# One-hot rows of the expert gates in four wide VectorE instructions, and six PSUM banks for the first expert product

## The chip, the cores and the metric

The kernel runs on one core of a Trainium2 chip. A core has a matrix engine (TensorE; PE in the rows, its weight loads PEld), three engines for elementwise work (VectorE or DVE, ScalarE or ACT, GpSimd or POOL) and a queue that issues DMAs (SyncE or SP). Each engine works through its own instructions strictly in order, and semaphores make one engine wait for another. Matmuls write to PSUM, which the kernel uses as eight banks of 128 x 512 float32. The metric is device time of the whole program in microseconds (us); lower is better.

## What is computed

The program is four layers one after another on 256 tokens of width 1024: a retention layer, a gated spatial layer, an attention layer and a delta-rule layer. The first two are each followed by a feed-forward layer with 16384 small experts, and the change lies in that feed-forward layer, which therefore runs twice. Cut to what matters:

```python
def peer_ffn(h, w_query, sub_keys, expert_u, expert_v):
    q = (ht @ w_query).reshape(T, 8, 2, 128)
    scores = einsum('thpd,hpkd->thpk', q, sub_keys)         # 128 keys per half
    s_top, i_top = top_k(scores, 16)
    cand = s_top[:, :, 0, :, None] + s_top[:, :, 1, None, :]
    best, pos = top_k(cand, 16)                             # 16 of 256 pairs per head
    expert_idx = i_top_0[a] * 128 + i_top_1[b]              # first index, second index
    gates = softmax(best)
    a = gelu(einsum('tkd,td->tk', expert_u[expert_idx], x)) * gates
    return einsum('tk,tkd->td', a, expert_v[expert_idx])
```

## The kernel before, in words

The kernel doesn't gather experts. It computes the product of the tokens with all 16384 rows of `expert_u` (the first expert product), multiplies by a gate matrix that is zero where an expert was not chosen, and multiplies by all of `expert_v` (the second). In `peer`, the first product is a loop over 128 blocks `i` of 128 experts. A block's weights are two **pieces** of four 128 x 128 tiles each. A piece arrives by DMA as float32 in `stage` (two buffers of four pieces each), is rounded by ScalarE to `whi` (line 143, "the cast"), and the remainder `wlo` is formed by VectorE, or by GpSimd for a part of the pieces (line 145). TensorE then makes three products per tile: `whi` with the tokens' high part, `whi` with their low part, `wlo` with their high part (lines 402 to 404). So a piece is 12 matmuls of 256 columns and a block is 24. A `stage` buffer is free for the next DMA when the last remainder of its four pieces is done. Eight pieces of `whi` and `wlo` can be held while the choice of experts runs, four afterwards (`closing.close()` gives back the extra buffers). GpSimd makes every second remainder up to there, then every fourth.

A block's sum lies in a PSUM bank, `acc`. ScalarE takes it out with a gelu to `gs` (line 1023), and every second block `gs` is spilled to DRAM. Before the change, `self.bank()` turns over two banks, `b0` and `b1`, so that the first matmul of a block needs the gelu of the block two before it. ScalarE's order for one block is: cast, cast, gelu, with the casts belonging to later blocks.

Beside the first product runs `choose`, a generator that is called for a little work after every block (`self.step`). It finds the top 16 of the scores and of the pairs, expands positions to indices with long bf16 operations of 2048 elements per partition (lines 931 to 940, "the expansion", once for each half of the tokens), and then builds the gate matrix four tokens at a time: 64 **groups** per layer, about six of them in every seven blocks. For a token, the gate matrix is a product of two one-hot matrices over its 128 choices: rows of the first index, and rows of the second index times the gate, the gate split in two float16 parts. In the kernel before that takes three VectorE instructions of 128 elements per token (lines 965 and 967), 12 per group, then eight matmuls of 128 columns (line 970) into a long-lived bank, and one ScalarE instruction that takes the bank out (line 972). `oh` has two buffers, so the first one-hot instruction of a group waits for the matmuls of the group two before. After the loop, the second product takes banks `b2` to `b5` for its sums.

The order on each engine is static: a scheduler lays the instructions down when the program is built, and may move a remainder in between one-hot instructions.

Of the kernel before, what the change touches and what calls it, by code (L numbers as in the profile page):

```python
# [14 lines left out]
HF = mybir.dt.float16  # L15
# [3 lines left out]
ALU = mybir.AluOpType  # L19
# [4 lines left out]
P = 128  # L24
D = 1024
KC = D // P
T = 256
# [25 lines left out]
NK = 128  # L53
# [268 lines left out]
class Kernel:  # L322
# [538 lines left out]
    def choose(self, scores, big, work, chosen, closing):  # L861

        nc = self.nc
        s16 = big.tile([P, 2, 16, TOPK], F32, tag="s16", name="s16")
        ix = big.tile([P, 2, 16, TOPK], U32, tag="ix", name="ix")
        i12 = chosen.tile([P, 2, T], HF, tag="i12", name="i12")
        gp = chosen.tile([P, 2, T], HF, tag="gp", name="gp")
# [9 lines left out]

        line = chosen.tile([P, NK], HF, tag="line", name="line")
        self.tc.keep_in_program_order(nc.vector.tensor_copy(line, self.const("iota")))
        for m in range(16):  # L880
            while m not in scores:
                yield -1
            for t in range(2):
                scratch = work.tile([P, P], F32, tag="scr", name="scr")
                self.top16(s16[:, t, m], ix[:, t, m], scores[m][:, t * P:(t + 1) * P], scratch)
                yield 1000
        ixb = big.tile([P, 2, 2, TOPK, PEER_H], BF, tag="ixb", name="ixb")
        nc.vector.tensor_copy(ixb, ix.rearrange("p t (h u) a -> p t u a h", u=2))
        iota = big.tile([P, TOPK, P], BF, tag="iota16", name="iota16")
# [3 lines left out]
        for t in range(2):  # L893
# [34 lines left out]
            for u in range(2):  # L928
# [4 lines left out]
                    op=ALU.is_equal)  # L933
                yield 1200
                nc.vector.tensor_tensor(eq, eq, ixb[:, t, u, :, None].to_broadcast([P, TOPK, TOPK, PEER_H]),
                                        op=ALU.mult)
# [22 lines left out]
        for t4 in range(T // 4):  # L959
            ts = slice(4 * t4, 4 * t4 + 4)  # L960
            acc = self.long_bank()
            oh = chosen.tile([P, 4, 3, NK], HF, tag="oh", name="oh", bufs=2)
            for u in range(4):
                t = slice(4 * t4 + u, 4 * t4 + u + 1)
                nc.vector.tensor_scalar(oh[:, u, 0], line, i12[:, 0, t], None, op0=ALU.is_equal)  # L965
                for w in range(2):
                    nc.vector.tensor_scalar(oh[:, u, 1 + w], line, i12[:, 1, t], gp[:, w, t], op0=ALU.is_equal,  # L967
                                            op1=ALU.mult)
                for w in range(2):
                    nc.tensor.matmul(acc[:, u * P:(u + 1) * P], oh[:, u, 0], oh[:, u, 1 + w], start=w == 0,  # L970
                                     stop=w == 1, skip_group_check=True)
            nc.scalar.activation(gates[:, :, ts], acc.rearrange("p (t i) -> p i t", t=4), AF.Copy,
                                 scale=1.0 / GATE_SCALE)
            yield 1400

    def peer(self, layer, later=()):
        nc = self.nc
        with ExitStack() as ctx:
            io = self.pool("peerio", bufs=2, ctx=ctx)
            chosen = self.pool("peersel", ctx=ctx)  # L980
# [27 lines left out]
            w = self.stream(f"peer_query{layer}", KC * 16)  # L1008
# [4 lines left out]
            self.rate = US  # L1013

            w = Weights(self, self.ins[f"peer_u{layer}"], NK * KC)
            for i in range(NK):
                acc = self.bank()[:, :T]
                for k in range(KC):
                    self.mm3(acc, w.tile(i * KC + k), (self.hi[:, k, :T], self.lo[:, k, :T]), k == 0, k == KC - 1)
                self.tick()  # L1020
                if i % 2 == 0:
                    gs = io.tile([P, 2 * T], F32, tag="gs", name="gs").rearrange("p (a b) -> p a b", a=2)
                nc.scalar.activation(gs[:, i % 2], acc, AF.Gelu_apprx_tanh)  # L1023
                if i % 2:
                    nc.scalar.dma_start(spill[i // 2], gs)
                self.step(self.rate)
# [4 lines left out]
            w = Weights(self, self.ins[f"peer_v{layer}"], NK * KC)  # L1031
# [4 lines left out]
            ts = slice(META, L) if layer else slice(0, T)  # L1036
# [6 lines left out]
            for i in range(NK):  # L1043
                if i % 2 == 0:

                    a = (io if i else chosen).tile([P, 2 * T], F32, tag="gs" if i else "oh", name="gs", bufs=2)
                    a = a.rearrange("p (a b) -> p a b", a=2)
# [679 lines left out]
```

## Time and profile before

| | |
|---|---|
| time, median of 3 runs | 3218.7 us (3213.13 to 3223.79) |
| the profiled execution | 3223.57 us, of which the span 3221.8 us |
| TensorE matmul busy | 3081.6 us, 96% of the span, granted clock 0.975 on average |
| VectorE busy | 2410.0 us, 75% |
| ScalarE busy | 1774.3 us, 55% |
| GpSimd busy | 526.2 us, 16% |
| first product, layer 0: first and last gelu start | 328.1 and 750.2 us |
| first product, layer 1 | 1439.4 and 1860.6 us |
| one-hot instructions, layer 0: first and last start | 427.0 and 725.2 us (line 965) |
| one-hot instructions, layer 1 | 1538.4 and 1835.7 us (line 965) |

Busy time of TensorE is modelled up to each matmul's end, and neighbouring matmuls overlap. Whether TensorE went at full pace is therefore better seen from the number of matmuls that a stretch holds than from its busy time. [...] VectorE's average over the span says little, since the stages differ: in the slices of the span that hold the one-hot instructions it is busy nine tenths or more.

### The profile page before, as it was taken

Reading aid. Unit: us, or ns where it says so; the run is one execution under the profiler, and the core shown is the slowest. Engines: PE = TensorE matmul, PEld = TensorE weight load, DVE = VectorE, ACT = ScalarE, POOL = GpSimd, SP = SyncE. Lnnn points to the kernel's source line nnn. Section 1 sums busy time; section 2 is a strip of 40 time slices with the busy share of each in tenths; the row PEclk is TensorE's granted clock in tenths of the full one; section 3 lists DMA queues with packets and bytes.
Section 4 is the critical chain, followed back from the end, with each engine's and each line's share of the span. In section 5 each row is a group of like instructions: output and inputs, shape, how many; then the busy total and the mean of one; then the engine's idle time right before and its main releaser. Section 6 shows DMA issues by size and latency. Waiting matters only on the chain. (4 is left out here: it accounts for less than half of the span.)

```text
span 3221.8 us, 63744 instructions
## 1 busy us (share of the span) xinstructions
PE 3081.6 (96%) x24317; PEld 2932.2 (91%) x24317; DVE 2410.0 (75%) x5694; ACT 1774.3 (55%) x3495; POOL 526.2 (16%) x476
## 2 busy tenths in 40 slices
PE   6999999999999999999999999999999998999998
PEld 5899999999999978999999999999677998898898
DVE  7777979996777687678899877666556965744783
ACT  4566555555555455555555555556456656824763
POOL 1213431110000003234321200000001001133101
PEclk8999999999999999999999999999899999989999
DMA  6655555558777765455555576665323543310453
GB/s 256 243 189 180 198 196 193 187 182 283 260 260 266 269 229 210 157 179 211 188 193 186 203 277 232 234 231 182 110 76 106 197 171 134 118 40 28 145 191 110
DMA packets 119779, 604.14 MB, mean 188 GB/s; under 512 B 14136, under 2 KB 15336, under 8 KB 61488
## 3 DMA queue, kind: packets, MB, share of 16 engines
q1 hardware_dynamic: 98496, 556.84, 48.8%
q10 hardware_dynamic: 19008, 35.72, 3.0%
q0 software_dynamic: 1968, 7.51, 0.7%
q8 instruction: 190, 3.11, 0.4%
q14 instruction: 117, 0.96, 0.1%
HBM read 565.38 MB, written 34.64 MB: 186 GB/s over the span
## 5 line engine op out<-in xcount | busy, mean ns | idle before, releaser
L402 PE MATMUL bank<-hi,whi 128*128 128x256 f32 (+1 forms) x5968 | 1725.4, 289 | 42.0 <-ACT gs L1023 17.5
L404 PE MATMUL bank<-hi,wlo 128*128 128x256 f32 (+1 forms) x5968 | 1707.5, 286 | 32.5 <-DVE wlo L145 30.2
L403 PE MATMUL bank<-lo,whi 128*128 128x256 f32 (+1 forms) x5968 | 1699.3, 285 | 1.2 <-DVE lo L379 1.2
L143 ACT CAST whi<-stage 128x512 fp32r<-128x512 f32 x1780 | 1077.0, 620 | 1051.7 <-PE bank L403 740.5
L145 DVE TENSOR_TENSOR wlo<-stage,whi 128x512 fp32r<-128x512 f32 x1566 | 1084.6, 707 | 468.0 <-ACT whi L143 452.1
L402 PEld LDWEIGHTS bank<-hi,whi 128*128 128x128 f32 x5968 | 1140.5, 191 | 62.1 <-ACT gs L1023 19.0
L404 PEld LDWEIGHTS bank<-hi,wlo 128*128 128x128 f32 x5968 | 1138.0, 191 | 52.2 <-DVE wlo L145 48.8
L403 PEld LDWEIGHTS bank<-lo,whi 128*128 128x128 f32 x5968 | 1139.0, 191 | 4.9 <-DVE lo L379 2.2
L145 POOL TENSOR_TENSOR wlo<-stage,whi 128x512 fp32r<-128x512 f32 x214 | 306.3, 1433 | 725.0 <-ACT whi L143 717.7
L967 DVE TENSOR_SCALAR oh<-line,i,gp 128x128 f16<-128x128 f16 x1024 | 337.5, 372 | 0.0
L403 PE MATMUL bank<-zl,whi 128*128 128x272 f32 (+1 forms) x736 | 211.3, 287 | 1.0 <-DVE zl L379 1.0
L402 PE MATMUL bank<-zh,whi 128*128 128x272 f32 (+1 forms) x736 | 211.7, 288 | 0.0
L404 PE MATMUL bank<-zh,wlo 128*128 128x272 f32 (+1 forms) x736 | 211.2, 287 | 0.0
L965 DVE TENSOR_SCALAR oh<-line,i 128x128 f16<-128x128 f16 x512 | 150.8, 295 | 0.0
L185 POOL TENSOR_TENSOR sqa<-sqa,sq 128x272 f32<-128x272 f32 (+1 forms) x36 | 30.0, 834 | 692.3 <-ACT sq L183 692.3
L403 PEld LDWEIGHTS bank<-zl,whi 128*128 128x128 f32 x736 | 140.2, 190 | 1.8 <-DVE zl L379 1.4
L402 PEld LDWEIGHTS bank<-zh,whi 128*128 128x128 f32 x736 | 140.1, 190 | 0.7 <-issue 0.4
L404 PEld LDWEIGHTS bank<-zh,wlo 128*128 128x128 f32 x736 | 139.8, 190 | 0.2 <-issue 0.2
L1049 DVE TENSOR_TENSOR gs<-gs,gates 128x512 f32<-128x512 f32 x128 | 88.1, 688 | 55.8 <-DMA gs<-spill 55.5
L1023 ACT ACTIVATE gs<-bank 128x256 f32<-128x256 f32 x256 | 96.8, 378 | 8.0 <-PE bank L404 7.9
L379 DVE TENSOR_TENSOR lo<-gs,hi 128x512 fp32r<-128x512 f32 x126 | 86.4, 686 | 0.4
L378 ACT CAST hi<-gs 128x512 fp32r<-128x512 f32 x126 | 77.9, 618 | 15.1 <-DVE gs L1049 15.0
(432 smaller groups left out, 3114.8 us busy)
## 6 DMA issues: line engine op xcount, KB each, us to landing
stage<-in_peer_u SPq DMA_DIRECT2D x128, 1024.0 KB, 4.8
stage<-in_peer_v SPq DMA_DIRECT2D x128, 1024.0 KB, 5.0
adaw<-in_ada_w SPq DMA_DIRECT2D x96, 512.0 KB, 4.9
stage<-in_ffn_up SPq DMA_DIRECT2D x44, 1024.0 KB, 4.8
spill<-gs ACTq DMA_DIRECT2D x128, 256.0 KB, 2.0
gs<-spill SPq DMA_DIRECT2D x128, 256.0 KB, 5.0
stage<-in_ffn_down SPq DMA_DIRECT2D x22, 1024.0 KB, 4.7
stage<-in_peer_query SPq DMA_DIRECT2D x16, 1024.0 KB, 4.8
```

The costliest lines, as they stand in the source:

```text
L143: k.nc.scalar.copy(hi, src)
L145: eng.tensor_tensor(lo, src, hi.bitcast(F32), op=ALU.subtract)
L185: k.nc.gpsimd.tensor_tensor(self.sum, self.sum, sq, op=ALU.add)
L378: self.nc.scalar.copy(hi, src)
L379: self.nc.vector.tensor_tensor(lo, src, hi.bitcast(F32), op=ALU.subtract)
L402: mm(acc, wh, xh, start=first, stop=False, skip_group_check=True)
L403: mm(acc, wh, xl, start=False, stop=False, skip_group_check=True)
L404: mm(acc, wl, xh, start=False, stop=last, skip_group_check=True)
L965: nc.vector.tensor_scalar(oh[:, u, 0], line, i12[:, 0, t], None, op0=ALU.is_equal)
L967: nc.vector.tensor_scalar(oh[:, u, 1 + w], line, i12[:, 1, t], gp[:, w, t], op0=ALU.is_equal, op1=ALU.mult)
L1023: nc.scalar.activation(gs[:, i % 2], acc, AF.Gelu_apprx_tanh)
L1049: nc.vector.tensor_tensor(a, a, self.gates[:, i:i + 2], op=ALU.mult)
```

## The change

Three edits, in `choose` and `peer`:

- A group's 12 one-hot instructions become four, each over 512 elements. The first makes the rows of the first index of all four tokens, token after token (dense). The second makes the rows of the second index with two tokens interleaved: element 2j is key j of the one token, element 2j+1 key j of the other. The third and the fourth multiply that by the two parts of the gate. All four are operations of two tensors (`tensor_tensor`), where the twelve had one tensor and scalars per partition (`tensor_scalar`).
- `rep` holds the key numbers 0, 0, 1, 1, ... for the interleaved comparison, made once per layer. The matmuls take the dense rows as weights as before; their moving operand now reads every second element.
- The first 124 blocks of the first product turn over six banks, `b0` to `b5`; the last four use `b0` and `b1`, since the second product takes the others.

```diff
         self.tc.keep_in_program_order(nc.vector.tensor_copy(line, self.const("iota")))
+        rep = chosen.tile([P, NK, 2], HF, tag="rep", name="rep")
+        self.tc.keep_in_program_order(
+            nc.vector.tensor_copy(rep, self.const("iota")[:, :, None].to_broadcast([P, NK, 2])))
...
-            oh = chosen.tile([P, 4, 3, NK], HF, tag="oh", name="oh", bufs=2)
-            for u in range(4):
-                t = slice(4 * t4 + u, 4 * t4 + u + 1)
-                nc.vector.tensor_scalar(oh[:, u, 0], line, i12[:, 0, t], None, op0=ALU.is_equal)
-                for w in range(2):
-                    nc.vector.tensor_scalar(oh[:, u, 1 + w], line, i12[:, 1, t], gp[:, w, t], op0=ALU.is_equal,
-                                            op1=ALU.mult)
-                for w in range(2):
-                    nc.tensor.matmul(acc[:, u * P:(u + 1) * P], oh[:, u, 0], oh[:, u, 1 + w], start=w == 0,
-                                     stop=w == 1, skip_group_check=True)
+
+            oh = chosen.tile([P, 4, 2, NK, 2], HF, tag="oh", name="oh", bufs=2)
+            pairs = lambda a: a[:, ts].rearrange("p (a b) -> p a b", b=2)[:, :, None, :].to_broadcast([P, 2, NK, 2])
+            first = oh[:, 0].rearrange("p a b c -> p (a b c)").rearrange("p (t i) -> p t i", t=4)
+            nc.vector.tensor_tensor(first, i12[:, 0, ts, None].to_broadcast([P, 4, NK]),
+                                    line[:, None].to_broadcast([P, 4, NK]), op=ALU.is_equal)
+            nc.vector.tensor_tensor(oh[:, 3], pairs(i12[:, 1]), rep[:, None].to_broadcast([P, 2, NK, 2]),
+                                    op=ALU.is_equal)
+            for w in range(2):
+                nc.vector.tensor_tensor(oh[:, 1 + w], oh[:, 3], pairs(gp[:, w]), op=ALU.mult)
+            for u, w in itertools.product(range(4), range(2)):
+                nc.tensor.matmul(acc[:, u * P:(u + 1) * P], first[:, u], oh[:, 1 + w, u // 2, :, u % 2],
+                                 start=w == 0, stop=w == 1, skip_group_check=True)
...
+            wide = itertools.cycle(f"b{i}" for i in range(6))
             for i in range(NK):
-                acc = self.bank()[:, :T]
+
+                acc = (self.bank() if i >= NK - 4 else self.bank(next(wide)))[:, :T]
```

Where it moves instructions, the places that matter are two. The first is VectorE in layer 0, in the middle of the groups. `wlo` rows are the remainders of the first product's weights, `oh` the one-hot rows. Before, from two remainders over one group to the next remainder:

```order
L145 TENSOR_TENSOR wlo_6055<-stage_6036,whi_6054 128x512
L965 TENSOR_SCALAR oh_6073<-line_3070,i12_3068 128x128
L967 TENSOR_SCALAR oh_6073<-line_3070,i12_3068,gp_3069 128x128 x2
L965 TENSOR_SCALAR oh_6073<-line_3070,i12_3068 128x128
L967 TENSOR_SCALAR oh_6073<-line_3070,i12_3068,gp_3069 128x128 x2
L965 TENSOR_SCALAR oh_6073<-line_3070,i12_3068 128x128
L967 TENSOR_SCALAR oh_6073<-line_3070,i12_3068,gp_3069 128x128 x2
L965 TENSOR_SCALAR oh_6073<-line_3070,i12_3068 128x128
L967 TENSOR_SCALAR oh_6073<-line_3070,i12_3068,gp_3069 128x128 x2
L145 TENSOR_TENSOR wlo_6097<-stage_6036,whi_6096 128x512
```

And now, at the same place of the pattern, a few groups earlier:

```order
L145 TENSOR_TENSOR wlo_5985<-stage_5982,whi_5984 128x512
L145 TENSOR_TENSOR wlo_6001<-stage_5982,whi_6000 128x512
L969 TENSOR_TENSOR oh_6019<-i12_3068,line_3070 128x512
L971 TENSOR_TENSOR oh_6019<-i12_3068,rep_3072 128x512
L974 TENSOR_TENSOR oh_6019<-oh_6019,gp_3069 128x512 x2
L145 TENSOR_TENSOR wlo_6035<-stage_5982,whi_6034 128x512
```

What a remainder has ahead of it in VectorE's queue is four instructions where it was twelve; how many groups stand between two remainders is the same.

The second place is TensorE in layer 0, the last block before the first group: the end of its first piece, the start of its second piece, and the start of the next block. In brackets is what a matmul waits for (Activation is ScalarE). Before:

```order
L404 MATMUL bank_5529<-hi_2192,wlo_5531 128x256
L402 MATMUL bank_5529<-hi_2192,whi_5546 128x256
L403 MATMUL bank_5529<-lo_2193,whi_5546 128x256
L404 MATMUL bank_5529<-hi_2192,wlo_5547 128x256 [waits Pool_49]
...
L402 MATMUL bank_5572<-hi_2192,whi_5575 128x256 [waits Activation_49]
L403 MATMUL bank_5572<-lo_2193,whi_5575 128x256
L404 MATMUL bank_5572<-hi_2192,wlo_5576 128x256 [waits DVE_49]
```

And now:

```order
L404 MATMUL bank_5531<-hi_2192,wlo_5533 128x256
L402 MATMUL bank_5531<-hi_2192,whi_5548 128x256 [waits Activation_49]
L403 MATMUL bank_5531<-lo_2193,whi_5548 128x256
L404 MATMUL bank_5531<-hi_2192,wlo_5549 128x256 [waits Pool_49]
...
L402 MATMUL bank_5574<-hi_2192,whi_5577 128x256 [waits Activation_49]
L403 MATMUL bank_5574<-lo_2193,whi_5577 128x256
L404 MATMUL bank_5574<-hi_2192,wlo_5578 128x256 [waits DVE_49]
```

Before, a block's first matmul waited for a gelu, which stands behind the casts of both of the block's pieces in ScalarE's order, and one wait covered all three. Now each piece waits for its own cast. The order of TensorE's, GpSimd's and SyncE's instructions is the same before and after; on ScalarE a cast and a copy of scores have changed places, once per layer, in the query projection, and VectorE's other instructions stand as they did but for some small ones around the expansion.

## Rows read from the trace of the kernel before

**Rows 1.** Windows: busy us and (count) per engine, granted clock, DMA share, GB/s.

```profile
330.00:370.00 40.00, 40.00 (x343) 40.00 (x342) 35.88 (x146) 21.64 (x44) 21.53 (x15) 1.00 0.59 207
370.00:410.00 40.00, 33.76 (x272) 33.14 (x271) 33.52 (x103) 19.06 (x37) 19.47 (x12) 0.96 0.59 212
440.00:470.00 30.00, 26.56 (x203) 26.21 (x202) 19.21 (x37) 10.18 (x22) 10.14 (x7) 0.89 0.53 182
490.00:725.00 235.00, 228.17 (x2075) 219.27 (x2074) 235.00 (x792) 130.60 (x260) 44.45 (x34) 1.00 0.53 187
1490.00:1520.00 30.00, 25.40 (x189) 24.79 (x189) 25.57 (x69) 14.23 (x27) 13.12 (x8) 0.89 0.54 195
1550.00:1580.00 30.00, 26.61 (x211) 26.33 (x211) 20.66 (x38) 10.81 (x23) 12.04 (x8) 0.94 0.52 181
1600.00:1835.00 235.00, 228.05 (x2075) 219.29 (x2074) 235.00 (x789) 130.43 (x259) 45.06 (x34) 1.00 0.53 187
```

**Rows 2.** Groups by line in 490 to 725 us: count | busy us, mean ns.

```profile
L967 DVE TENSOR_SCALAR oh<-line,i,gp 128x128 f16<-128x128 f16 x462 | 152.5, 373 | 0.0
L145 DVE TENSOR_TENSOR wlo<-stage,whi 128x512 fp32r<-128x512 f32 x99 | 65.7, 690 | 0.0
L145 POOL TENSOR_TENSOR wlo<-stage,whi 128x512 fp32r<-128x512 f32 x34 | 45.7, 1344 | 191.1 <-ACT whi L143 191.1
L970 PE MATMUL bank<-oh 128*128 128x128 f16 x464 | 38.3, 220 | 0.2
```

**Rows 3.** Timeline of TensorE around one group: start us, us, instruction.

```profile
606.05 0.62 PE L970 MATMUL bank<-oh 128*128 128x128 f16 x8
606.48 0.36 PE L402 MATMUL bank<-hi,whi 128*128 128x256 f32 x1
606.68 0.28 PE L403 MATMUL bank<-lo,whi 128*128 128x256 f32 x1
```

**Rows 4.** Waits of TensorE, 370 to 470 and 1490 to 1580 us: total, times, longest.

```profile
PE bank L402 <- ACT gs L1023: 9.7, 4, 3.9
...
PE bank L402 <- ACT gs L1023: 7.9, 3, 3.5
```

**Rows 5.** Waits of the weight loads, 490 to 725 us.

```profile
PEld bank L404 <- DVE wlo L145: 11.4, 23, 0.8
```

**Rows 6.** Timeline of ScalarE in a stall; in brackets idle time and its end.

```profile
402.47 1.14 ACT L143 CAST whi<-stage 128x512 fp32r<-128x512 f32 x2 [7.16 <-DMA stage<-in_peer_u]
403.52 0.38 ACT L1023 ACTIVATE gs<-bank 128x256 f32<-128x256 f32 x1
```

**Rows 7.** Timeline of TensorE in the same stall.

```profile
403.94 0.58 PE L402 MATMUL bank<-hi,whi 128*128 128x256 f32 x1 [3.87 <-ACT gs L1023]
```

**Rows 8.** Timeline of GpSimd: the expansion, and one remainder amid the groups.

```profile
389.06 8.49 POOL L145 TENSOR_TENSOR wlo<-stage,whi 128x512 fp32r<-128x512 f32 x4 [5.60 <-ACT whi L143]
...
565.26 1.35 POOL L145 TENSOR_TENSOR wlo<-stage,whi 128x512 fp32r<-128x512 f32 x1 [6.16 <-ACT whi L143]
```

**Rows 9.** Timeline of VectorE: in the stall, beside GpSimd's remainder, one whole group.

```profile
400.70 0.68 DVE L145 TENSOR_TENSOR wlo<-stage,whi 128x512 fp32r<-128x512 f32 x1
403.29 0.68 DVE L145 TENSOR_TENSOR wlo<-stage,whi 128x512 fp32r<-128x512 f32 x1
...
565.28 1.60 DVE L967 TENSOR_SCALAR oh<-line,i,gp 128x128 f16<-128x128 f16 x2
...
609.41 0.24 DVE L965 TENSOR_SCALAR oh<-line,i 128x128 f16<-128x128 f16 x1
609.58 0.53 DVE L967 TENSOR_SCALAR oh<-line,i,gp 128x128 f16<-128x128 f16 x2
...
611.84 1.29 DVE L145 TENSOR_TENSOR wlo<-stage,whi 128x512 fp32r<-128x512 f32 x2
```

**Rows 10.** Two-tensor instructions on bf16: a group in 400 to 430 us; line 935, min/median/max ns.

```profile
L939 DVE TENSOR_TENSOR eq<-eq 128x512 bf16<-128x512 bf16 x2 | 0.8, 414 | 0.0
...
L935 DVE TENSOR_TENSOR eq<-eq,ixb x8: 1210/1215/2314, 392.4 to 1557.3; 128x2048 bf16<-128x2048 bf16 x8
```

## The prediction

> **What bounds the kernel now.** I read the page first: TensorE is busy 96% of the span, so a change elsewhere pays only where TensorE runs below its pace. The edits act on the first expert product alone, so the second view is the windows over it, read by the count of matmuls, since busy times of matmuls overlap. In a quiet stretch of the first product, 40 us hold 343 matmuls of 256 columns: 0.1166 us each, 1.40 us a piece (12), 2.80 us a block (24) [rows 1]. Against that pace two kinds of stretch fall short, in both layers alike.
>
> The choice phase: the windows from 370, 440, 1490 and 1550 us hold 272, 203, 189 and 211 matmuls, where the pace gives 343, 257, 257 and 257 [rows 1]. That is 71, 54, 68 and 46 missing, 239 in all, or 27.9 us. The waits there name the cause for most of it: the first matmul of a block waits for the gelu that empties its bank, 9.7 us in layer 0 and 7.9 us in layer 1 [rows 4]. The rest is the clock: its share of 0.96, 0.89, 0.89 and 0.94 [rows 1] costs 1.6 + 3.3 + 3.3 + 1.8 = 10.0 us. TensorE had stood still before those low levels, so I count them to the same stalls.
>
> The group phase: 490 to 725 us and 1600 to 1835 us each hold 2075 matmuls [rows 1], of which 464 belong to groups, 58 groups [rows 2]. A group takes 0.43 us from its first matmul to the next block's, and that block's first step is 0.20 us instead of 0.12 [rows 3], so 0.51 us. At full pace: 1611 x 0.1166 + 58 x 0.51 = 217.4 us. The stretch lasts 235, so 17.6 us are lost per layer. The waits name the remainder `wlo` (11.4 us of standing weight loads in 23 waits [rows 5], and each stop costs a restart too). VectorE is busy all 235.00 us there [rows 1]: it is the bound of this phase, with TensorE close behind.
>
> So 27.9 + 2 x 17.6 = 63 us is all that these two edits can find.
>
> **Edit 1, the one-hot rows.** Per six groups (seven blocks) TensorE needs 217.4 / 58 x 6 = 22.5 us and takes 24.3. VectorE's work in that time: a group is 2.43 us, from 609.41 to the next remainder at 611.84 [rows 9]; six are 14.6. Remainders: 99 per 58 groups [rows 2], so 10.2, each 0.60 from start to start (two take 1.29 us, one alone 0.69 [rows 2, 9]), 6.1 us. GpSimd's remainders: 34 [rows 2], so 3.5; while one runs, VectorE's pair of one-hot instructions takes 1.60 us instead of 0.53 [rows 8, 9], so 1.07 each, 3.8 us. Sum 24.5 us against 24.3 measured: the account closes.
>
> The new group is four instructions of 512 float16 elements from two tensors. No row shows them. The nearest rows bound each: 414 ns when two elements go through at a time (bf16, two tensors, 512 elements [rows 10]) and 690 ns when one goes (float32 [rows 2]); with the 0.09 us by which neighbours overlap, 0.33 and 0.60 us. Line 935 repeats a short row of one operand many times, as the new comparison and multiplications do, and takes 1215 ns for 2048 elements, the fast rate [rows 10]; so I take 0.33 for these three. The dense one repeats a single element 128 times, which no row does for two tensors of 16 bits; I take the slow 0.60. The first multiplication needs the comparison's result, 0.1 us more. A group: 0.60 + 3 x 0.33 + 0.1 = 1.7 us; the ends are 1.3 (all fast) and 2.4 (all slow), the latter just what it costs now.
>
> [...]
>
> With 1.7, VectorE's load is 10.2 + 6.1 + 3.8 = 20.1 us in TensorE's 22.5, 89%. The point from which the edit helps fully is (22.5 - 9.9) / 6 = 2.1 us. The load isn't far below one, and the queue is in order: a remainder may find a whole group (1.7), GpSimd's hold (1.07), its cast (0.62) and itself (0.69) in its way, 4.1 us, where the four held pieces give it 3 x 1.40 + 0.51 = 4.7. It fits, narrowly; so I take three quarters of 17.6, 13 us per layer, **26 us**. What is late next is TensorE itself. A group that finds its buffer not yet released holds up the remainders behind it, but the buffer comes free two groups earlier than needed, some 5.5 us ahead of the next remainder in TensorE's order; nothing for that. `rep` is one small instruction per layer, hidden in the choice phase where TensorE doesn't wait for VectorE.
>
> TensorE's moving operand now takes every second float16, one per 4 bytes. The first product's float32 columns are one per 4 bytes too, 256 in 0.1166 us, and a group's dense columns go at 0.43 / 8 = 54 ns per 128, the same rate [rows 1, 3]. So nothing is added; the other end is a rival below.
>
> **Edit 2, six banks.** The stall at 400 us as an example: ScalarE waits 7.16 us for a weight DMA with a cast at its head, the gelu behind it starts at 403.52 [rows 6], and TensorE goes on at 403.94 after 3.87 us idle [rows 7]. The DMA is late because `stage` came free late: GpSimd took 8.49 us for four remainders during the expansion [rows 8]. But eight pieces are held here, and the four next pieces were ready: the last remainder on VectorE among them started at 400.70 and took 0.68 [rows 9]. With six banks TensorE needs no gelu of the last two blocks, so it runs on from 400.1 for 4 x 1.40 us to 405.7, and the piece behind the late DMA has its remainder at 403.29 + 0.68 = 403.97 [rows 9]. The stall goes wholly, with 1.7 us to spare. All seven stalls are at most 3.9 us [rows 4], below the 5.6 us of four pieces, so I take nearly all of 27.9: **24 us**. If the pieces weren't ready, it would be about nothing.
>
> **Sum.** 24 + 26 = 50 us. The profiled execution took 3223.6 us (1.8 of it outside the span); it stands 4.9 above the median of the runs. 3223.6 - 50 = 3173.6, and against the median 3168.7: I say **3169 us**.
>
> **Rivals.**
> - *No pairs.* If the three interleaved instructions go one element at a time, a group costs 2.4 us and VectorE stays the bound: only the banks pay, 3218.7 - 24 = 3195. Against it: line 935's rate [rows 10]. For it: its repeated rows are 8 long, the new ones 2. Chance 0.12.
> - *Banks in vain.* Without the gelu TensorE soon stops at the next late cast or remainder, as GpSimd's and VectorE's queue in the expansion is unchanged: 3218.7 - 26 = 3193. For it: the 7.16 us wait for the DMA stays [rows 6]. Against it: the margin of 1.7 us. Chance 0.09.
> - *No effect.* Both together: within 10 us of the time now. Chance 0.05.
> - *Slower: the strided columns.* If a column with a gap is read at a fraction of the rate, each of 1024 group matmuls, on TensorE's own path, grows. At half rate a group costs 0.43 more; six 2.6, TensorE 25.1 us per six groups where it takes 24.3 now, and the banks' 24 us make up for it. The point from which it decides is 24.3 + 24 / (2 x 58 / 6) = 25.5 us, 3.0 us above 22.5, 63 ns per matmul. At a third, 0.86 more: 27.7 us, 3.4 x 21 - 24 = 47 us slower, 3266. Against it: float32 columns cover the same bytes per column [rows 1, 3]. Chance 0.04.
>
> **How the numbers follow.** The forecast has 0.70, with 3153 (all 63 us, and a fast run) to 3185 as its own range. The range reaches on to the two one-sided cases, with 2 us for the runs' spread: 3153 to 3197; what lies outside is no effect, slower, and the tails. About 0.3% (10 us) is what a measurement of this kernel can tell from no change. Faster by more than that: 0.70 + 0.12 + 0.09 = 0.91; the same 0.05; slower 0.04.
>
> **What would show it.** The wait of the blocks' first matmul for the gelu falls from 17.6 us to under 3, and the clock stays at 1.00 through the choice phase. The weight loads' wait for `wlo` falls from 11.4 us per layer to under 5; VectorE is no longer busy all through the groups; the dense instruction takes near 690 ns and the other three near 414; eight group matmuls still take 0.43 us. The prediction is wrong if the interleaved ones take 690 too, if waits for `whi` or `wlo` take the gelu's place in the choice phase, or if the group's matmuls spread out.

## The result, and the profile after

The changed kernel takes 3178.5 us (median of 4 runs, 3171.71 to 3188.25) where the kernel before took 3216.9 beside it (4 runs): a ratio of 0.9883, 95% interval 0.9862 to 0.9903, that is 38 us less (31 to 44). The profiled execution of after took 3171.71 us, 3169.9 of it the span: the shortest of its runs, where that of before was the longest of its own. The two spans are 52 us apart, so some of what their rows differ by is not the change's.

The windows that tell most are those over the two stretches that fell short before: the choice phase (330 to 460 us in layer 0, 1430 to 1560 in layer 1) and the groups (460 to 700, 1560 to 1790). Windows of the kernel before, cut this way; columns as in [rows 1], and the first count is that of the matmuls:

```profile
330.00:460.00 130.00, 120.31 (x983) 119.35 (x982) 111.10 (x376) 66.10 (x129) 62.87 (x41) 0.96 0.58 205
460.00:700.00 240.00, 234.28 (x2134) 226.32 (x2133) 230.16 (x766) 131.89 (x263) 47.57 (x35) 1.00 0.53 188
...
1430.00:1560.00 130.00, 122.39 (x1007) 121.50 (x1005) 111.84 (x389) 68.25 (x133) 57.28 (x40) 0.97 0.59 206
1560.00:1790.00 230.00, 224.28 (x2017) 217.20 (x2018) 218.96 (x721) 125.09 (x251) 50.30 (x36) 0.99 0.53 188
```

The same windows of the kernel after:

```profile
330.00:460.00 130.00, 123.62 (x1034) 123.02 (x1034) 110.25 (x347) 65.12 (x131) 63.70 (x42) 0.99 0.60 212
460.00:700.00 240.00, 240.00 (x2255) 237.33 (x2253) 209.75 (x360) 141.23 (x281) 59.35 (x37) 1.00 0.56 199
...
1430.00:1560.00 130.00, 125.69 (x1061) 125.19 (x1060) 109.81 (x328) 66.37 (x134) 61.43 (x39) 0.99 0.59 211
1560.00:1790.00 230.00, 230.00 (x2156) 227.41 (x2155) 201.20 (x343) 135.24 (x270) 56.94 (x35) 1.00 0.56 199
```

In the groups 121 and 139 more matmuls fit into the same time. As the groups begin earlier on TensorE, 48 and 72 of them belong to 6 and 9 groups more that the windows hold; the other 140 at 0.1166 us and the 15 groups at 0.51 make 24.0 us. VectorE is busy 209.75 of 240 us instead of 230.16, and TensorE has no idle time there in the list of waits. In the choice phase it is 51 and 54 more, 24 of which are three groups in layer 1: 11.0 us. There 81 of the 1115 that the pace gives in 130 us are still missing in layer 0. The waits of TensorE from 320 to 720 us show for what:

```profile
PE bank L404 <- DVE wlo L145: 5.9, 2, 3.8
```

The gelu of [rows 4] is gone from this list. A remainder stands in its place, though not at as many stops: two of them here, and two of 4.3 us in all in layer 1.

The groups by line, 460 to 700 us of after; each row answers to one of [rows 2]:

```profile
L145 DVE TENSOR_TENSOR wlo<-stage,whi 128x512 fp32r<-128x512 f32 x109 | 72.3, 685 | 17.8 <-ACT whi L143 17.7
L971 DVE TENSOR_TENSOR oh<-i,rep 128x512 f16<-128x512 f16 x62 | 60.0, 969 | 0.0
L145 POOL TENSOR_TENSOR wlo<-stage,whi 128x512 fp32r<-128x512 f32 x37 | 59.8, 1617 | 180.2 <-ACT whi L143 180.2
L974 DVE TENSOR_TENSOR oh<-oh,gp 128x512 f16<-128x512 f16 x124 | 47.2, 422 | 2.1
L969 DVE TENSOR_TENSOR oh<-i,line 128x512 f16<-128x512 f16 x62 | 42.7, 688 | 10.2 <-PE bank L976 10.2
L976 PE MATMUL bank<-oh 128*128 128x128 f16 x504 | 39.9, 220 | 0.0
```

The last row in the same window of before:

```profile
L970 PE MATMUL bank<-oh 128*128 128x128 f16 x456 | 37.4, 220 | 0.1
```

The dense instruction (969) takes 688 ns, the interleaved multiplications (974) 422. The interleaved comparison (971) has a mean of 969, but over the whole trace its median is 420: those that meet GpSimd make up the difference (last section). VectorE now waits, for TensorE to release `oh` and for ScalarE's casts: it has time to spare.

### The profile page after: what moved, and what is told of

The parts are those of the page before. It is cut to its first block, busy times and chain, and to the rows that moved or that the text cites. A ratio compares the mean times of both kernels' runs of the same rounds, so it can differ in the third digit from the quotient of the medians.

```text
span 3169.9 us, 62720 instructions
## 1 busy us (share of the span) xinstructions
PE 3052.1 (96%) x24317; PEld 2918.0 (92%) x24317; DVE 2326.1 (73%) x4672; ACT 1766.5 (56%) x3495; POOL 545.4 (17%) x476
## 5 line engine op out<-in xcount | busy, mean ns | idle before, releaser
L145 DVE TENSOR_TENSOR wlo<-stage,whi 128x512 fp32r<-128x512 f32 x1566 | 1096.3, 714 | 470.6 <-ACT whi L143 457.3
L145 POOL TENSOR_TENSOR wlo<-stage,whi 128x512 fp32r<-128x512 f32 x214 | 327.0, 1532 | 660.3 <-ACT whi L143 653.1
L971 DVE TENSOR_TENSOR oh<-i,rep 128x512 f16<-128x512 f16 x128 | 119.5, 934 | 0.0
L969 DVE TENSOR_TENSOR oh<-i,line 128x512 f16<-128x512 f16 x128 | 90.7, 708 | 20.0 <-PE bank L976 20.0
L974 DVE TENSOR_TENSOR oh<-oh,gp 128x512 f16<-128x512 f16 x256 | 97.7, 422 | 4.2
```

The costliest lines, as they stand in the source:

```text
L145: eng.tensor_tensor(lo, src, hi.bitcast(F32), op=ALU.subtract)
L969: nc.vector.tensor_tensor(first, i12[:, 0, ts, None].to_broadcast([P, 4, NK]), line[:, None].to_broadcast([P, 4, NK]), op=ALU.is_equal)
L971: nc.vector.tensor_tensor(oh[:, 3], pairs(i12[:, 1]), rep[:, None].to_broadcast([P, 2, NK, 2]), op=ALU.is_equal)
L974: nc.vector.tensor_tensor(oh[:, 1 + w], oh[:, 3], pairs(gp[:, w]), op=ALU.mult)
```

## Experiments

Two terms are to be told apart, the one-hot rows and the banks, and then why the banks gave less than the prediction had for them. The first theory is the prediction's own: each edit pays in its phase, 26 and 24 us. Its rivals: the banks are in vain because the next late remainder stops TensorE anyway; and the interleaving is not needed, since fewer instructions would do as much.

**One edit alone.** The first kernel is after with two banks:

```diff
-            wide = itertools.cycle(f"b{i}" for i in range(6))
...
-                acc = (self.bank() if i >= NK - 4 else self.bank(next(wide)))[:, :T]
+                acc = self.bank()[:, :T]
```

> The changed kernel with the first product back on two banks, so the one-hot edit alone. Theory A (each edit cures its own phase): the group phase runs at TensorE's pace as in the changed kernel, so the 17.6 us per layer lost there come back, and the waits of a block's first matmul for the gelu stay near 17 us in all: about 3217 - 33 = 3184 us. Theory B (the banks carry the gain, since a block that need not wait for a gelu lets TensorE ride over late work in the group phase too): the group phase stays short of the pace, about 3217 - 12 = 3205 us.

Measured: 3192.2 us (6 runs), ratio 0.9915 (0.9893 to 0.9938), 27 us less than before (20 to 34). Windows of this kernel:

```profile
330.00:460.00 130.00, 121.57 (x994) 120.95 (x993) 110.31 (x369) 67.98 (x132) 62.80 (x42) 0.96 0.59 208
460.00:700.00 240.00, 240.00 (x2241) 237.45 (x2240) 200.84 (x346) 138.38 (x275) 58.18 (x37) 1.00 0.56 199
```

The groups run as in after (2241 matmuls), the choice phase as in before (994), and the wait for the gelu is still 16.1 us over the whole trace. That is theory A, though 8 us above its 3184: it has the whole 17.6 us per layer come back, and the count shows 24 us for both (why, in the next section).

The second is the kernel before with the six banks:

```diff
+            wide = itertools.cycle(f"b{i}" for i in range(6))
...
-                acc = self.bank()[:, :T]
+                acc = (self.bank() if i >= NK - 4 else self.bank(next(wide)))[:, :T]
```

> The kernel before with six banks for the first 124 blocks, nothing else. Theory A: the group phase keeps its 235 us (VectorE is the bound), the gelu waits go, but a part of the choice phase's 28 us comes back as waits for the remainder wlo, as in the changed kernel: about 3217 - 10 = 3207 us. Theory B: about 3217 - 26 = 3191 us.

Measured: 3204.7 us (12 runs), ratio 0.9969 (0.9954 to 0.9984), 10 us less (5 to 15). Its windows, and its first row of TensorE's waits over the whole trace, ahead of the same row of before:

```profile
330.00:460.00 130.00, 124.08 (x1026) 123.62 (x1026) 111.17 (x368) 63.72 (x129) 61.81 (x41) 0.97 0.59 210
460.00:700.00 240.00, 233.63 (x2129) 225.43 (x2127) 236.34 (x789) 133.97 (x266) 47.62 (x36) 1.00 0.53 190
```

```profile
PE bank L404 <- DVE wlo L145: 42.1, 54, 4.1
```

```profile
PE bank L404 <- DVE wlo L145: 30.2, 49, 4.2
```

The gelu's row is gone from the list, and the wait for `wlo` has become 42.1 us from 30.2: about 12 of the 17.5 us that the gelu took came back as another wait. The groups stay as they were. The edits add up: 27 + 10 = 37 against 38 for both.

**Is the interleaving needed?** After with the second index dense as well: still four instructions of 512 elements, all of which repeat a single element of one operand.

```diff
-            nc.vector.tensor_tensor(oh[:, 3], pairs(i12[:, 1]), rep[:, None].to_broadcast([P, 2, NK, 2]),
-                                    op=ALU.is_equal)
+            rows = [oh[:, n].rearrange("p a b c -> p (a b c)").rearrange("p (t i) -> p t i", t=4) for n in range(4)]
+            nc.vector.tensor_tensor(rows[3], i12[:, 1, ts, None].to_broadcast([P, 4, NK]),
+                                    line[:, None].to_broadcast([P, 4, NK]), op=ALU.is_equal)
...
-                nc.vector.tensor_tensor(oh[:, 1 + w], oh[:, 3], pairs(gp[:, w]), op=ALU.mult)
+                nc.vector.tensor_tensor(rows[1 + w], rows[3], gp[:, w, ts, None].to_broadcast([P, 4, NK]),
+                                        op=ALU.mult)
...
-                nc.tensor.matmul(acc[:, u * P:(u + 1) * P], first[:, u], oh[:, 1 + w, u // 2, :, u % 2],
+                nc.tensor.matmul(acc[:, u * P:(u + 1) * P], first[:, u], rows[1 + w][:, u],
```

> The changed kernel with the rows of the second index dense too: still four instructions of 512 elements, but the comparison and the two multiplications repeat one element 128 times instead of pairs. Theory A (the rate of the elements counts): each takes about 690 ns, a group 4 x 0.60 + 0.1 = 2.5 us, above the 2.1 us that TensorE's pace allows; VectorE is the bound again and the group phase is back at about 235 us or a little over: about 3178 + 32 = 3210 us. Theory B (the number of instructions ahead of a remainder counts): still four, so about 3178 us. Either way the eight matmuls of a group take 0.43 us, if a gap between columns costs nothing.

Measured: 3217.2 us (10 runs), ratio 0.9999 (0.9985 to 1.0014): no gain at all, and 7 us above the 3210 of theory A. A window of its groups, and the timeline of VectorE over one group that meets no GpSimd:

```profile
460.00:700.00 240.00, 225.13 (x2072) 218.32 (x2070) 237.57 (x330) 130.29 (x258) 49.06 (x33) 1.00 0.52 183
```

```profile
559.34 0.68 DVE L969 TENSOR_TENSOR oh<-i,line 128x512 f16<-128x512 f16 x1
559.94 0.68 DVE L972 TENSOR_TENSOR oh<-i,line 128x512 f16<-128x512 f16 x1
560.66 1.29 DVE L975 TENSOR_TENSOR oh<-oh,gp 128x512 f16<-128x512 f16 x2
561.87 1.28 DVE L145 TENSOR_TENSOR wlo<-stage,whi 128x512 fp32r<-128x512 f32 x2
```

The groups are slower than in the kernel before: 2072 matmuls against 2134, and 1976 against 2017 in layer 1, 12 us lost. From 559.34 to 561.87 a group is 2.53 us, against 2.43 before [rows 9]; 0.10 us on 128 groups is 13 us. That eats what the banks bring in the choice phase (67 and 50 matmuls, 13.6 us). So the interleaving is what pays; four instructions for twelve, by themselves, are slightly slower, and theory B, by which their number counts, is out.

**Why the banks gave little.** In the choice phase of after, TensorE's longest stop is the 3.8 us shown above. The timeline of TensorE there:

```profile
391.05 0.28 PE L403 MATMUL bank<-lo,whi 128*128 128x256 f32 x1
395.09 0.39 PE L404 MATMUL bank<-hi,wlo 128*128 128x256 f32 x1 [3.76 <-DVE wlo L145]
```

That of VectorE ahead of it (934 and 938 are the expansion, lines 931 and 935 of before):

```profile
386.71 4.45 DVE L934 TENSOR_TENSOR eq<-place,iota 128x2048 bf16<-128x2048 bf16 x2
391.08 2.29 DVE L938 TENSOR_TENSOR eq<-eq,ixb 128x2048 bf16<-128x2048 bf16 x1
393.29 1.75 DVE L145 TENSOR_TENSOR wlo<-stage,whi 128x512 fp32r<-128x512 f32 x1
```

And that of GpSimd:

```profile
386.51 7.98 POOL L145 TENSOR_TENSOR wlo<-stage,whi 128x512 fp32r<-128x512 f32 x4 [7.57 <-ACT whi L143]
```

While GpSimd makes its four remainders, VectorE's long instructions take 2.2 to 2.3 us each instead of the 1.21 of [rows 10], and the remainder that TensorE needs stands behind three of them. So the new theory: the choice phase is lost to GpSimd's help, not to the banks. Against it stands that VectorE, without that help, would have more remainders to make and be later still. The constant at line 43 says how often a remainder goes to GpSimd in the query projection (but for its first products, which have a constant of their own) and the choice phase; at 0 VectorE makes them all:

```diff
-RELIEF = 2
+RELIEF = 0
```

> The changed kernel with all remainders on VectorE up to the group phase (GpSimd makes none in the query projection and the choice phase). Theory A (the stall that is left in the choice phase comes from GpSimd's remainders, which stretch the expansion's instructions on VectorE by about 1.1 us each): the expansion takes half as long, the waits for wlo in the choice phase fall below 2 us per layer, about 3178 - 12 = 3166 us. Theory B (a remainder is late because it stands behind the expansion in VectorE's order, and VectorE with every remainder has more in front of it): the waits stay or grow, 3178 to 3190 us.

Measured: 3164.5 us (4 runs), ratio 0.9832 (0.9806 to 0.9859), 54 us less than before (45 to 62). A window, then all instructions of line 934 (min/median/max ns):

```profile
330.00:460.00 130.00, 129.77 (x1112) 129.28 (x1111) 119.53 (x405) 69.12 (x140) 2.98 (x2) 1.00 0.63 220
```

```profile
L934 DVE TENSOR_TENSOR eq<-place,iota x8: 1211/1224/1248, 385.4 to 1515.6; 128x2048 bf16<-128x2048 bf16 x8
```

The choice phase runs near the pace (1112 matmuls, 22 of them of the first groups, where the pace gives 1115), with the clock at 1.00, though VectorE makes more remainders in it. That is theory A (3166 expected). The order has changed too; the expansion on VectorE begins so:

```profile
385.38 1.23 DVE L934 TENSOR_TENSOR eq<-place,iota 128x2048 bf16<-128x2048 bf16 x1
386.52 1.28 DVE L145 TENSOR_TENSOR wlo<-stage,whi 128x512 fp32r<-128x512 f32 x2
387.73 1.22 DVE L938 TENSOR_TENSOR eq<-eq,ixb 128x2048 bf16<-128x2048 bf16 x1
```

Two remainders stand behind its first long step, where after has three long steps ahead of the first.

The same constant in the kernel before, with neither edit:

> The kernel before with no remainders on GpSimd before the group phase, nothing else: 12 one-hot instructions per group, two banks. Theory A: the choice phase loses little, the group phase stays bound by VectorE: about 3217 - 20 = 3197 us. Theory B: about 3217 us.

Measured: 3193.6 us (5 runs), ratio 0.9923 (0.9897 to 0.9948), 25 us less (17 to 33). Its windows, and TensorE's wait for the gelu over the whole trace:

```profile
330.00:460.00 130.00, 127.10 (x1065) 126.27 (x1064) 116.70 (x414) 68.15 (x135) 1.29 (x1) 0.99 0.62 221
460.00:700.00 240.00, 232.64 (x2120) 224.13 (x2119) 240.00 (x804) 132.71 (x265) 45.57 (x34) 1.00 0.52 187
```

```profile
PE bank L402 <- ACT gs L1023: 5.7, 5, 2.1
```

With two banks the choice phase gains more than six banks brought it (1065 matmuls, 8 of them of a group, against 1026), and the wait for the gelu falls to 5.7 us from 17.5: with the number of banks as it was, most of that wait disappears together with GpSimd's help. The groups keep their old loss, VectorE busy all 240 us. Then the one-hot rows with `RELIEF = 0` and two banks:

> The one-hot edit, no remainders on GpSimd before the group phase, and two banks as before the change. Theory A (the choice phase's stalls all begin with GpSimd's remainders, which stretch the expansion on VectorE, free stage late and make the next weights late): the gelu waits shrink from 16 us to the ones at the two table switches per layer, some 1 to 2 us each, and the time is within 8 us of the same kernel with six banks, 3164 to 3172 us. Theory B (with two banks a late cast always holds a gelu up, so banks and relief are two separate cures): the gelu waits stay above 10 us and the time is about 3164 + 20 = 3184 us.

Measured: 3165.3 us (6 runs), ratio 0.9823 (0.9797 to 0.9849), 57 us less (49 to 65): as fast as with six banks, within the runs' spread. TensorE still waits for the gelu, over the whole trace:

```profile
PE bank L402 <- ACT gs L1029: 5.0, 3, 2.7
```

Theory B, which left more than 10 us of that wait, is out.

And after with no remainder on GpSimd in the groups either (`RELIEF = 0`, and `RELIEF_G = 0` at line 44 instead of 4):

> The changed kernel with no remainders on GpSimd in the choice phase nor in the group phase. Theory A (with the new one-hot rows TensorE itself is the bound of the group phase, and GpSimd's remainders are covered): the same as with GpSimd in the group phase alone, 3164 us within 5. Theory B (they still cost, as about sixty of them per layer pair stretch the second one-hot instruction by 1.1 us): some 3164 - 8 us. If VectorE is pushed over TensorE's time by the remainders it takes over, some 10 us slower.

Measured: 3158.4 us (6 runs), ratio 0.9812 (0.978 to 0.9843), 61 us less (51 to 71). It is the fastest by its median, but its interval overlaps most of those of the two kernels with `RELIEF = 0` and the one-hot rows, so it can't be told from them. What it changes in the groups is seen in line 971, over the whole trace:

```profile
L971 DVE TENSOR_TENSOR oh<-i,rep 128x512 f16<-128x512 f16 x128 | 53.6, 419 | 0.0
```

Its mean is now the median of after. The groups don't get faster by it (2247 matmuls in 460 to 700 us): TensorE was their bound already.

**Does a gap cost TensorE anything?** After with the first index interleaved too, so that the weights as well are every second element:

```diff
-            first = oh[:, 0].rearrange("p a b c -> p (a b c)").rearrange("p (t i) -> p t i", t=4)
-            nc.vector.tensor_tensor(first, i12[:, 0, ts, None].to_broadcast([P, 4, NK]),
-                                    line[:, None].to_broadcast([P, 4, NK]), op=ALU.is_equal)
+            nc.vector.tensor_tensor(oh[:, 0], pairs(i12[:, 0]), rep[:, None].to_broadcast([P, 2, NK, 2]),
+                                    op=ALU.is_equal)
...
-                nc.tensor.matmul(acc[:, u * P:(u + 1) * P], first[:, u], oh[:, 1 + w, u // 2, :, u % 2],
+                nc.tensor.matmul(acc[:, u * P:(u + 1) * P], oh[:, 0, u // 2, :, u % 2], oh[:, 1 + w, u // 2, :, u % 2],
```

> The changed kernel with the rows of the first index interleaved by two tokens as well, so that all four instructions take pairs and TensorE's weight loads read every second element. VectorE's group falls from 1.7 to about 1.4 us, which is worth nothing where TensorE is the bound. Theory A (a gap between weights costs nothing, as one between columns doesn't): 3178 us, within 5. Theory B (a weight load with gaps takes twice as long or more, 96 to about 190 ns, and sets the pace of a group's eight matmuls): a group takes 0.3 us or more longer, 128 groups, 3178 + 40 us.

Measured: 3173.3 us (4 runs), ratio 0.9866 (0.9833 to 0.99), 43 us less than before (32 to 54), which can't be told from after. Its weight loads of the groups (min/median/max ns):

```profile
L975 PEld LDWEIGHTS <-oh x1024: 96/97/100, 459.7 to 1793.3; 128*128 128x128 f16 x171
```

Those of after:

```profile
L976 PEld LDWEIGHTS <-oh x1024: 94/96/101, 462.3 to 1794.9; 128*128 128x128 f16 x171
```

Weights with gaps load in the same time, so the dense first index is not needed.

**All in one table.** Work of TensorE gained over the kernel before, in us, from the four windows above and two ahead of them, which end in the query projection (150 to 330 and 1250 to 1430 us). A matmul that belongs to no group is priced at 0.1166 us, a group's eight at 0.51:

| kernel | query projection | choice phase | groups | sum | measured |
|---|---|---|---|---|---|
| one-hot rows alone | 0.6 | -0.3 | 24.0 | 24 | 27 (20 to 34) |
| six banks alone | 2.6 | 7.9 | -0.5 | 10 | 10 (5 to 15) |
| both: after | 4.2 | 11.0 | 24.0 | 39 | 38 (31 to 44) |
| after, all dense | 2.3 | 13.6 | -12.4 | 4 | 0 (-5 to 5) |
| after, both interleaved | 1.6 | 14.1 | 24.1 | 40 | 43 (32 to 54) |
| `RELIEF = 0` alone | 6.6 | 16.9 | -2.5 | 21 | 25 (17 to 33) |
| one-hot rows, `RELIEF = 0` | 6.6 | 16.8 | 23.8 | 47 | 57 (49 to 65) |
| after, `RELIEF = 0` | 7.3 | 24.8 | 23.8 | 56 | 54 (45 to 62) |
| after, `RELIEF = 0`, `RELIEF_G = 0` | 6.5 | 25.5 | 23.9 | 56 | 61 (51 to 71) |

The columns are as good as independent: the one-hot rows alone move the groups, the banks and the help alone the choice phase, the help the stretch ahead of it too. In the first column the kernels with `RELIEF = 2` differ by up to 3.6 us, though no edit of theirs acts there: that is how much profiled executions differ by themselves. One sum lies outside its interval, that of the one-hot rows with `RELIEF = 0`, whose profiled execution (3175.3 us) was the slowest of its six. One thing stays open. With `RELIEF = 0`, the six banks show 8 us more in the choice phase (24.8 against 16.8), and the median times don't show it; with intervals of 8 us to either side, they may hide it.

## Why the prediction was right, and where not

- **The bound.** That the groups are bound by VectorE and the choice phase by late weights held: the first went with a shorter group alone, the second with timelier remainders alone.
- **The one-hot rows.** 26 us predicted, 27 measured alone and 24.0 by the count in after. A group on VectorE, 460 to 700 us of after:

```profile
601.96 0.68 DVE L969 TENSOR_TENSOR oh<-i,line 128x512 f16<-128x512 f16 x1
602.56 0.42 DVE L971 TENSOR_TENSOR oh<-i,rep 128x512 f16<-128x512 f16 x1
603.01 0.77 DVE L974 TENSOR_TENSOR oh<-oh,gp 128x512 f16<-128x512 f16 x2
603.70 0.68 DVE L145 TENSOR_TENSOR wlo<-stage,whi 128x512 fp32r<-128x512 f32 x1
```

  From 601.96 to 603.70 it is 1.74 us, where the prediction had 1.7; both bounds that it chose from [rows 2, 10], 0.60 and 0.33 with the overlap, are met. For 512 elements the instruction that repeats one element takes 688 ns, those that repeat pairs 420. VectorE's load came out at 87% (209.75 of 240), predicted 89%. One step was right in its size but not in its reason: a quarter of the 17.6 us per layer was taken off for collisions in VectorE's queue. There were none that reached TensorE. What is missing is TensorE's own pace. The timeline of after from one group over a block to the next:

```profile
597.25 0.63 PE L976 MATMUL bank<-oh 128*128 128x128 f16 x8
597.69 0.36 PE L402 MATMUL bank<-hi,whi 128*128 128x256 f32 x1
600.61 0.63 PE L976 MATMUL bank<-oh 128*128 128x128 f16 x8
```

  The group's 0.51 us holds: 0.44 to the block's first matmul, and that one's 0.20 [rows 3] for 0.12. The other 23 take (600.61 - 597.69 - 0.20) / 23 = 0.1183 us each, not 0.1166; on the 1751 in the 240 us that is 3 us per layer, most of the quarter (4.4 us). In part the 0.1166 was too short: the 343 that it is counted from include those that only reach into the 40 us. Why the pace in the groups is slower still is open.
- **The banks: the mis-sized term.** 24 us predicted, 10 measured alone, 11 by the count in after and as the difference of the two kernels. The step that failed is "the stall goes wholly, with 1.7 us to spare". It was worked out for the stall at 400 us with all that came before it left as it was. With six banks TensorE stops 22 matmuls ahead of that place, at a remainder that was no stop before. The same matmul in before (by its count back from the first group), and the remainder that it needs:

```profile
397.34 0.28 PE L404 MATMUL bank<-hi,wlo 128*128 128x256 f32 x1
```

```profile
394.62 1.77 DVE L145 TENSOR_TENSOR wlo<-stage,whi 128x512 fp32r<-128x512 f32 x1
```

  There the remainder was done at 396.4 us, about 1 us before TensorE came. In after TensorE is 6.2 us earlier (391.2): the two gelu waits ahead of that place are gone, 2.9 us with their restarts (idle 0.98 and 1.40 us, and 0.5 more up to the second matmul after each), and it was 3.3 us ahead already when the first product began. The remainder is only 1.4 us earlier (395.0). The margin was that of a TensorE held up. The rival "banks in vain" had the mechanism (the next late remainder) and went wrong only in that it left nothing of the gain.
- **The sum.** 50 us predicted, 38 (31 to 44) measured; the banks' term, 13 to 14 us too large, accounts for the difference, and for the 9 us between 3169 and 3178. That the time lies in the range all the same is owed to the one-hot rows and to a range that reaches to the cases in which one of the edits brings nothing; the working of the banks' term has no part in it.
- **The rivals.** "No pairs" was priced with all four slow at 2.4 us, break-even; the dense kernel shows 2.53. The price left out the 0.1 us for a result that the next instruction needs (in the dense kernel 0.72 from 559.94 to 560.66 us, against 0.60 for the step before), which the forecast's own group has, and with it a little is lost. "The strided columns" is out, by the timeline of TensorE above: eight matmuls take 0.44 us to the next block's first (597.25 to 597.69), 0.43 before [rows 3].
- **The signs named.** The gelu's wait falls as said, but the clock doesn't hold in the choice phase (0.99 on average; 0.57 from 396 to 400 us, just after TensorE had stood still for 3.76). The sign against, a wait for `wlo` in the gelu's place, came in part. In the groups the signs came as named: no weight load waits for `wlo` between 460 and 700 us, and VectorE has idle time.
- **What wasn't considered** is the cause itself. The prediction names GpSimd's 8.49 us [rows 8] as the reason for the late DMA, and then treats that as given. Removing it, one constant, is worth 25 us by itself, more than twice the banks. Two things change with it, and no run here separates them: VectorE's and GpSimd's instructions no longer stretch each other (line 934 takes 1.22 us in the median, 2.23 in after), and the scheduler puts remainders behind the first long step of the expansion instead of the third. An estimate for the stop in layer 0: at 1.14 us a step (385.38 to 386.52 in the kernel with `RELIEF = 0`) the three of after would end at 386.71 + 3 x 1.14 = 390.1 and the remainder at 390.8, just ahead of TensorE at 391.2. So the stretch alone would be enough for it, which is not shown.

The best kernels here are those with the one-hot rows and no help from GpSimd in the choice phase: 3158 to 3165 us, with six banks or with two.

## What to carry to other kernels

A stall's margin holds only for the arrival time that it was read at: when an edit removes several stalls in a row, walk the engine through them again from its earlier arrival before taking the sum. Work handed to a helper engine wasn't free here for the one that it helps (1.21 us became 2.2 to 2.3); when both run longer side by side, try the kernel without the help first. Long two-tensor instructions paid here in place of many short ones only with the repeated operands of most of them laid out in pairs (a group of 1.74 us; 2.53 all dense, 2.43 before).

## What the runs showed of the hardware

Of the four new instructions it is mostly the interleaved comparison that meets GpSimd: over the whole trace of after line 971 has a mean of 934 ns and a median of 420, lines 969 and 974 means of 708 and 422 and medians of 687 and 421. VectorE in after, at such a place:

```profile
604.65 0.69 DVE L969 TENSOR_TENSOR oh<-i,line 128x512 f16<-128x512 f16 x1 [0.27 <-PE bank L976]
605.26 1.52 DVE L971 TENSOR_TENSOR oh<-i,rep 128x512 f16<-128x512 f16 x1
```

And GpSimd:

```profile
604.81 1.69 POOL L145 TENSOR_TENSOR wlo<-stage,whi 128x512 fp32r<-128x512 f32 x1 [5.05 <-ACT whi L143]
```

The instruction that was running when GpSimd's began keeps its 0.69 us; the next takes 1.52 instead of 0.42 and ends 0.28 us after GpSimd's, and GpSimd's own takes 1.69 where [rows 8] have 1.35. That it costs both sides (1.1 us here, 0.3 there) was not expected. That TensorE reads every second float16 in the time of dense ones, as columns (0.44 us for eight matmuls, 0.43 before) and as weights (97 ns against 96), was the other thing that no row of the kernel before showed.
